# Sixteen accumulating DMAs of a fused encoder block, issued at other places in the program

## The chip, the cores and the metric

The kernel runs on one core of one Trainium2 chip. The metric is the device time of one execution in microseconds (us), and of several executions the median. The core has a matrix engine (TensorE, PE in the profile; its weight loads are shown apart as PEld), three engines for elementwise work (VectorE or DVE, ScalarE or ACT, GpSimd or POOL), and SyncE (SP), which here only issues DMAs. Each engine works through its own queue of instructions in order and waits at semaphores for the others. A DMA is issued from the queue of SP, ACT or POOL and then moved by 16 DMA engines.

## The reference

One layer of an encoder on 512 tokens of width 1024, in float32:

```python
xn = rmsnorm(x, norm_mix_g)
u  = xn @ w_in                       # q | k | v | xr | gr | ga | gb, 1024 columns each
ya = chunked_band_attention(q, k, v, rel_table) @ w_attn_out
yb = (rg_lru(conv(xr)) * gelu(gr)) @ w_rnn_out
h  = x + (sigmoid(ga) * ya + sigmoid(gb) * yb) @ w_o
g, up = split(rmsnorm(h, norm_ffn_g) @ w_ffn_in)     # 2816 columns each
h  = h + (silu(g) * up) @ w_ffn_out
out = rmsnorm(h, final_norm_g)
```

## The kernel before

**Products.** Every float32 product is made of three matmuls (`mm3`, L80 to L82): each operand is split into a rounded high part and a low part, and high by high, high by low and low by high are added up in PSUM. For weights, which come from HBM in blocks of 512 KB, `split` (L84) makes the two parts: ACT copies the high part (L86), then DVE subtracts it from the original (L87), and only then can the matmuls of L81, which read the low part, run.

**Stages in order.** Projections of `w_in` with the recurrence beside them; attention, head by head for 16 heads (`scores`, `transposed`, `weigh`, loop at L1155); the merge, which projects by `w_attn_out` in eight steps (`po_ya`, loop at L1174); the product with `w_o`; the FFN's first projection; the FFN's last projection and the final norm. From `v_all` on PE's order is the program's own.

**The FFN's first projection** runs in six units, `fg0`, `fu0`, `fg1`, `fu1`, `fg2`, `fu2`: the gate and the up columns of three groups (1024, 1024 and 768 columns each). A unit is a seven-product form of a two by two block product (Strassen-Winograd), in the order w11, t1, t2, w22, t3, w21, t4, each of 24 matmuls. The kinds that begin with t multiply sums of weight blocks, which DVE makes at L386, L401 and L407 from blocks that SP loads (L380). A weight of a product is in two halves u=0 and u=1; the matmuls of u=1 begin with the seventh of the product. The weight tiles `whl` have room for two products, so the halves of the next product are made while PE works on this one. Results that are needed again are kept by ACT in SBUF (`kept`, L1310; tiles `keep`, x1, z1 and x2). In the u units DVE adds them to a later bank in place (L1325) and POOL multiplies the sum by the gate (L1326). In the g units ACT applies SiLU (L1319). In `fg1`, `fg2` and the end PE transposes the finished gate products in between (`turn`, L1334).

**The weight sums of the last projection.** The last projection takes the same form over the 2048 rows of `w_ffn_out` that belong to `paired`, which is four groups of two row blocks. Its weight sums are not made on DVE: they are made in DRAM, by DMAs. Per group and kind (t1, t3, t2, t4) `out_copy` (L222, L224) copies a 512 KB block of `w_ffn_out` into a DRAM tile `out_t` from SP's queue, and `out_add` (L226) adds another one to it by an accumulating DMA of 512 KB from POOL's queue (L233). For t1 and t3 what is added is a block of `w_ffn_out`; for t2 it is the finished t1, for t4 the finished t2. That makes 16 copies and 16 adds; `adds` (L236) lists them in the order t1, t3 by groups, then the four t2, then the four t4. The sums are read back (L258 to L267) in the last projection only.

**Where the adds stand.** `step(adds, n, after=...)` (L238) takes the next n from the list. With `after`, `out_add` first has POOL copy one column of the named tile into a small `cell` (L230), and both are kept in the program's order, so that the add is not issued before the tile is there. Before the change four adds are issued in the attention, behind the heads of `ADDS_AT` (no `after`); four in the merge, one with each of its first four steps (L1181, after the tile `mT`); four in `fg1`, behind its products w11, t1, t2 and w22 (`spare_work`, L1419, which asks `ADDS` for the unit and `after` at L1437 for the tile); and four in `fg2` in the same way. The tiles of `after` are the first halves of x1, z1, x2 and of the gate `sg[0, 1]`.

Of the kernel before, what the change touches and what calls it, by code (L numbers as in the profile page):

```python
# [33 lines left out]
N_PLAIN = 3  # L34
GROUP = 2
COPIES = [1] * 16
ADDS_AT = (9, 11, 13, 15)
ADDS = {"fg1": 1, "fg2": 1}
PAIR_TILES = 2 * (11 - N_PLAIN) - (4 - (N_PLAIN - 1))


# [1 line left out]
def block_kernel(ctx: ExitStack, tc: tile.TileContext, x, norm_mix_g, w_in, b_merge, rel_table,  # L43
# [28 lines left out]
    def f(ap):  # L72
        return ap.bitcast(F32)

    def mm_tile(name, tag="mm"):
        return ps.tile([P, S], F32, tag=tag, bufs=4 if tag == "mm" else 2, name=name)
# [7 lines left out]
    def split(hi, lo, src):  # L84

        act.activation(hi, src, AF.Copy)  # L86
        dve.tensor_sub(lo, src, f(hi))  # L87

    def split_pair(o, src):
        split(o[:, 0], o[:, 1], src)  # L90
# [145 lines left out]
    adds = [(out_add, kind, g) for kinds in (("t1", "t3"), ("t2",), ("t4",)) for g in groups for kind in kinds]  # L236

    def step(todo, n=1, **more):  # L238

        for _ in range(min(n, len(todo))):  # L240
            what, *of = todo.pop(0)
            what(*of, **more)
# [207 lines left out]
    def weights(name, ahead=1):  # L450
        prefetch(index[name] + 1 + ahead)
        if index[name] + 1 == len(made):
            low_parts()
        return made[index[name]]

    def project(o, whl, c, xs, lo=0, hi=S):

        n = len(xs)
        for k in range(n):
            at = slice(c * P, (c + 1) * P)  # L460
            mm3(o[:, lo:hi], whl(0, k, at), whl(1, k, at),
                xs[k][:, 0, lo:hi], xs[k][:, 1, lo:hi], k == 0, k == n - 1)
# [80 lines left out]
    def features(pl, tag, name):  # L543

        t = pl.tile([P, KT, 2, S], F32R, tag=tag, name=name)
        return t, [t[:, k] for k in range(KT)]
# [606 lines left out]
    with tc.manual_schedule(engines={mybir.EngineType.PE}):  # L1153
        v_all(sums)
        for h in range(HEADS):  # L1155
# [5 lines left out]
            step(copies, COPIES[h])  # L1161
            if h in ADDS_AT:
                step(adds)
# [6 lines left out]
    m_all, mT = features(xnp, "xn", "mT")  # L1170
# [3 lines left out]
    for j in range(KT):  # L1174
        py = mm_tile(f"po_ya{j}")
        project(py, weights(f"ya{j - j % 2}", 2 if j >= 4 else 1), j % 2, aT)
        dve.scalar_tensor_tensor(ta[j], ta[j], 1.0, py[:], ALU.add, ALU.mult)
        dve.tensor_add(ta[j], ta[j], zB[j])
        at = low_ if j < 4 else every
        split(mT[j][:, 0, at], mT[j][:, 1, at], ta[j][:, at])  # L1180
        step(adds, j < 8 - len(ADDS_AT), after=f(mT[j][:, 0, 0:1]))  # L1181
        if j < 4:
            s3 = tg_.tile([P, 256], F32, tag="tg", name=f"ms3_{j}")
            dve.tensor_sub(s3[:], ta[j][:, low_], ta[j][:, high_])
            split(msT[j][:, 0, high_], msT[j][:, 1, high_], s3[:])
        else:
            i = j - 4
            dve.tensor_add(ta[j][:, high_], ta[i][:, high_], ta[j][:, high_])
            dve.tensor_sub(ta[i][:, low_], ta[j][:, high_], ta[i][:, low_])
            dve.tensor_sub(ta[j][:, low_], ta[j][:, low_], ta[i][:, low_])  # L1190
            split_pair(msT[j], ta[j])
            split(msT[i][:, 0, low_], msT[i][:, 1, low_], ta[i][:, low_])
# [226 lines left out]
    def spare_work(kind):  # L1419
        if unit in ADDS and kind in after:  # L1420
            step(adds, ADDS[unit], after=after[kind])

    for unit in f_units[1:]:
# [13 lines left out]
        after = {"w11": x1[0][:, 0:1], "t1": z1[0][:, 0:1], "t2": x2[0][:, 0:1], "w22": sg[0, 1][:, 0:1]}  # L1437
# [299 lines left out]
```

## Time and profile before

| what | value |
|---|---|
| time, median of 3 runs | 847.2 us |
| the 3 runs | 847.09, 847.20, 848.59 us |
| the profiled execution's own time | 848.82 us |
| its span, first to last instruction | 847.0 us |
| mean granted clock of TensorE | 0.997 |
| DVE, ACT, POOL busy in the span | 654.1, 524.3, 159.9 us |
| DMA, moved in the span | 153.96 MB |

Busy times are of one profiled execution. A row of the timeline gives the start in the span, the length, the engine, the line, the operation, the tile that is written and those that are read, and in brackets the idle time of the engine before it with what ended it. A row of the view by windows gives, for a stretch of the span, the busy time of PE, PEld, DVE, ACT and POOL with the number of instructions, the granted clock, the mean busy share of the 16 DMA engines and GB/s. Buffer numbers are left out of names in the profile, so `keep_fu_x` is x1 or x2 of any u unit, and `out_t` is any of the DRAM tiles.

### The profile page before, as it was taken

How to read it: one execution, taken by the hardware profiler on the slowest of the kernel's cores; microseconds unless marked ns; L12 is line 12 of the kernel's file. 1: busy time of each engine (PE TensorE's matmuls, PEld its weight loads, DVE VectorE, ACT ScalarE, POOL GpSimd, SP SyncE). 2: the span in 40 equal slices, each digit the busy share in tenths (PEclk: the TensorE clock that was granted, in tenths of full speed). 3: DMA queues.
4: the chain of work that ended last, by engine and by line, in shares of the span. 5: the costliest groups of instructions: out<-in, count | busy, mean ns of one | idle time of the engine just before them, and what ended most of it. 6: DMA issues, size and time to landing. Idle time of an engine off the chain costs nothing.

```text
span 847.0 us, 11664 instructions
## 1 busy us (share of the span) xinstructions
PE 837.2 (99%) x4102; PEld 708.8 (84%) x4102; DVE 654.1 (77%) x960; ACT 524.3 (62%) x868; POOL 159.9 (19%) x207
## 2 busy tenths in 40 slices
PE   9999999999999999999999999999999999999996
PEld 6988888888878888888888888888888999988885
DVE  6667779886999778777568777889777878599784
ACT  7595848773456678878544469663765466555543
POOL 2412030221040043343211000005102322200000
PEclk9999999999999999999999999999999999999998
DMA  8433386687565444549448984555955576455442
GB/s 286 166 103 117 130 298 243 212 271 243 167 205 150 132 134 148 157 152 223 94 132 211 320 294 154 157 187 166 229 176 159 150 187 207 140 177 168 160 165 99
DMA packets 104058, 153.96 MB, mean 182 GB/s; under 512 B 8024, under 2 KB 62896, under 8 KB 103488
## 3 DMA queue, kind: packets, MB, share of 16 engines
q1 hardware_dynamic: 99040, 141.32, 51.2%
q0 software_dynamic: 3728, 8.96, 6.4%
q10 hardware_dynamic: 1232, 2.95, 0.9%
q8 instruction: 32, 0.52, 0.3%
q14 instruction: 26, 0.21, 0.1%
HBM read 139.53 MB, written 30.45 MB: 201 GB/s over the span
## 4 chain that ended last, share of the span: by engine, by line
PE 84%; DVE 7%; ACT 4%; DMA 3%; issue 2%; ACTq 0%; DVEq 0%
PE fu_x L80 2%; PE fu_x L81 2%; PE fu_x L82 2%; PE o L1122 2%; PE fg_x L82 2%; PE fg_x L80 2%; PE fg_x L81 2%; PE pT L1102 2%; PE po_ga L82 2%; PE po_ya L80 2%; PE po_ya L82 2%; PE p_out L81 2%; PE p_out L80 2%; PE po_ya L81 2%; PE p_out L82 2%
## 5 line engine op out<-in xcount | busy, mean ns | idle before, releaser
L1326 POOL TENSOR_TENSOR sg<-sg,keep_fu_x 128x512 f32<-128x512 f32 (+1 forms) x10 | 17.8, 1784 | 163.4 <-DVE keep_fu_x L1325 163.4
L1091 POOL TENSOR_SCALAR p<-p,rl 128x128 f32<-128x128 f32 (+3 forms) x61 | 43.8, 733 | 13.7 <-DVE rl L1087 9.4
L1085 DVE CUSTOM_DVE_ANT_0 p<-s,bias 128x128 f32<-128x128 f32 (+1 forms) x64 | 28.6, 486 | 12.6 <-PE s L1077 11.1
L1086 ACT ACTIVATE p<-p,m 128x128 f32<-128x128 f32 (+1 forms) x64 | 35.5, 555 | 2.3 <-DVE m L1085 2.0
L87 DVE TENSOR_TENSOR whl_fu_w<-raw_fu_w,whl_fu_w 128x1024 fp32r<-128x1024 f32 (+1 forms) x18 | 22.1, 1230 | 9.0 <-ACT whl_fu_w L86 9.0
L87 DVE TENSOR_TENSOR pp<-pT,pp 128x384 fp32r<-128x384 f32 (+1 forms) x48 | 26.9, 595 | 2.0 <-ACT pp L86 1.8
L81 PE MATMUL po_xr<-xnT,whl_xr 128*128 128x512 f32 (+1 forms) x80 | 27.7, 354 | 0.0
L87 DVE TENSOR_TENSOR whl_fu_t<-t_fu,whl_fu_t 128x1024 fp32r<-128x1024 f32 (+1 forms) x18 | 23.2, 1293 | 5.9 <-ACT whl_fu_t L86 5.7
L81 PE MATMUL po_gr<-xnT,whl_gr 128*128 128x512 f32 (+1 forms) x80 | 27.5, 347 | 0.0
L82 PE MATMUL po_gr<-xnT,whl_gr 128*128 128x512 f32 (+1 forms) x80 | 27.3, 347 | 0.0
L82 PE MATMUL po_xr<-xnT,whl_xr 128*128 128x512 f32 (+1 forms) x80 | 27.3, 347 | 0.0
L80 PE MATMUL po_gr<-xnT,whl_gr 128*128 128x512 f32 (+1 forms) x80 | 27.2, 347 | 0.0
L738 POOL MEMSET bias<- 64x64 f32 x16 | 2.5, 155 | 130.7 <-DMA bias<-ext_d 130.7
L80 PE MATMUL po_xr<-xnT,whl_xr 128*128 128x512 f32 (+1 forms) x80 | 26.3, 352 | 0.4 <-ACT xnT L649 0.4
L86 ACT ACTIVATE whl_fu_w<-raw_fu_w 128x1024 fp32r<-128x1024 f32 (+1 forms) x18 | 17.7, 987 | 13.0 <-issue 7.1
L80 PE MATMUL po_k<-xnT,whl_qk 128*128 128x512 f32 x64 | 25.5, 398 | 0.0
L80 PE MATMUL po_q<-xnT,whl_qk 128*128 128x512 f32 x64 | 25.5, 398 | 0.0
L80 PE MATMUL po_ga<-xnT,whl_ga 128*128 128x512 f32 x64 | 25.5, 398 | 0.0
L80 PE MATMUL po_gb<-xnT,whl_gb 128*128 128x512 f32 x64 | 25.3, 395 | 0.0
L86 ACT ACTIVATE whl_fu_t<-t_fu 128x1024 fp32r<-128x1024 f32 (+1 forms) x18 | 17.7, 989 | 12.2 <-PE fu_x L82 8.9
L82 PE MATMUL po_ga<-xnT,whl_ga 128*128 128x512 f32 x64 | 25.1, 392 | 0.1
L81 PE MATMUL po_q<-xnT,whl_qk 128*128 128x512 f32 x64 | 25.0, 390 | 0.0
(610 smaller groups left out, 3036.8 us busy)
## 6 DMA issues: line engine op xcount, KB each, us to landing
raw_qk<-in_w_in_dram SPq DMA_DIRECT2D x32, 256.0 KB, 3.3
out_t<-in_w_ffn_out_dram SPq DMA_DIRECT2D x16, 512.0 KB, 5.5
raw_fu_w<-in_w_ffn_in_dram SPq DMA_DIRECT2D x16, 512.0 KB, 4.7
raw_fo<-in_w_ffn_out_dram SPq DMA_DIRECT2D x14, 512.0 KB, 4.3
raw_t<-out_t SPq DMA_DIRECT2D x24, 256.0 KB, 3.3
raw_xr<-in_w_in_dram SPq DMA_DIRECT2D x8, 512.0 KB, 6.0
raw_gr<-in_w_in_dram SPq DMA_DIRECT2D x8, 512.0 KB, 4.5
raw_ga<-in_w_in_dram SPq DMA_DIRECT2D x8, 512.0 KB, 4.9
```

Source lines behind the costliest of these rows:

```text
L80: pe.matmul(o, sh, mh, start=start, stop=False, skip_group_check=parts)
L81: pe.matmul(o, sh, ml, start=False, stop=False, skip_group_check=parts)
L82: pe.matmul(o, sl, mh, start=False, stop=stop, skip_group_check=parts)
L86: act.activation(hi, src, AF.Copy)
L87: dve.tensor_sub(lo, src, f(hi))
L738: pool.memset(b[64:128, 448:512], NEG)
L1085: dve.tensor_tensor_reduce(prob[qb][:], scs[qb][:, 0:w], bias[:, S - w:S], -1.0, 3e38, ALU.add, ALU.min, nmax[:, qb:qb + 1])
L1086: act.activation(prob[qb][:], prob[qb][:], AF.Exp, bias=nmax[:, qb:qb + 1], scale=-1.0, accum_out=lsum[:, qb:qb + 1])
L1091: eng.tensor_scalar(prob[qb][:], prob[qb][:], rl[:, qb:qb + 1], 1.0, ALU.mult, ALU.mult)
L1102: pe.transpose(pt[:, at * P:(at + 1) * P], prob[qb][:, kb * P:(kb + 1) * P], ident[:])
L1122: pe.matmul(po[:, S - n:S], st, pp[i][:, part, lo:lo + n], start=kb == 0 and part == 0, stop=kb == NT - 1 and part == 1)
L1326: (pool if keep and (unit != f_units[-1] or side) else dve).tensor_mul(o, o, keep[a] if keep else banks[a])
```

## The change

```diff
-ADDS_AT = (9, 11, 13, 15)
-ADDS = {"fg1": 1, "fg2": 1}
+ADDS_AT = ()
+ADDS = {"fu0": 1, "fg1": 1, "fu1": 1, "fg2": 1}
...
-        step(adds, j < 8 - len(ADDS_AT), after=f(mT[j][:, 0, 0:1]))
+        step(adds, 0, after=f(mT[j][:, 0, 0:1]))
```

The 16 adds stay what they are and keep their order in the list. No add is left in the attention or in the merge. `fu0` and `fu1` issue four adds each as well, behind their w11, t1, t2 and w22. So `fu0` now holds t1 and t3 of the first two groups, `fg1` those of the last two, `fu1` the four t2, and `fg2` the four t4 as before. PE's rows and SP's rows are the same and in the same order; on ACT and DVE a few neighbours change places in the merge.

POOL's queue in the attention before, from head 13's probabilities on (`p` is a head's probabilities, `bias` its bias tile):

```order
L1091 TENSOR_SCALAR p_2_3826<-p_2_3826,rl_3823 128x384
L233 DMA out_t_3_94<-in_w_ffn_out_dram 256x1x512
L738 MEMSET bias_4021 64x64
L1091 TENSOR_SCALAR p_0_3932<-p_0_3932,rl_3931 128x128
L1091 TENSOR_SCALAR p_1_3933<-p_1_3933,rl_3931 128x256
```

And now at the same place:

```order
L1091 TENSOR_SCALAR p_2_3825<-p_2_3825,rl_3822 128x384
L738 MEMSET bias_4019 64x64
L1091 TENSOR_SCALAR p_0_3930<-p_0_3930,rl_3929 128x128
L1091 TENSOR_SCALAR p_1_3931<-p_1_3931,rl_3929 128x256
L1091 TENSOR_SCALAR p_2_3932<-p_2_3932,rl_3929 128x384
```

The add is gone from between the probabilities.

POOL's queue in `fu0` before (`sg` is the gate of a token block, `keep_fu_x` and `keep_fu_z` the sums that DVE made in place):

```order
L1326 TENSOR_TENSOR sg_0_4935<-sg_0_4935,keep_fu_x_5294 128x512
L1326 TENSOR_TENSOR sg_1_4936<-sg_1_4936,keep_fu_x_5294 128x512
L1326 TENSOR_TENSOR sg_2_4937<-sg_2_4937,keep_fu_z_5295 128x512
L1326 TENSOR_TENSOR sg_3_4938<-sg_3_4938,keep_fu_z_5295 128x512
L1326 TENSOR_TENSOR sg_0_4935<-sg_0_4935,keep_fu_x_5293 128x512
L1326 TENSOR_TENSOR sg_1_4936<-sg_1_4936,keep_fu_x_5293 128x512
```

And now, in the same unit:

```order
L230 COPY cell_t_3_5312<-keep_fu_x_5277 128x1
L233 DMA out_t_3_92<-in_w_ffn_out_dram 256x1x512
L230 COPY cell_t_3_5355<-keep_fu_z_5279 128x1
L233 DMA out_t_3_94<-in_w_ffn_out_dram 256x1x512
L230 COPY cell_t_5_5394<-keep_fu_x_5278 128x1
L233 DMA out_t_5_96<-in_w_ffn_out_dram 256x1x512
L1326 TENSOR_TENSOR sg_0_4919<-sg_0_4919,keep_fu_x_5278 128x512
L1326 TENSOR_TENSOR sg_1_4920<-sg_1_4920,keep_fu_x_5278 128x512
L230 COPY cell_t_5_5437<-sg_0_4919 128x1
L233 DMA out_t_5_98<-in_w_ffn_out_dram 256x1x512
L1326 TENSOR_TENSOR sg_2_4921<-sg_2_4921,keep_fu_z_5279 128x512
L1326 TENSOR_TENSOR sg_3_4922<-sg_3_4922,keep_fu_z_5279 128x512
```

Three cells and adds stand ahead of the first product with the gate, and one of each behind the second.

POOL's queue in `fu1` now, where before only the six products stood:

```order
L230 COPY cell_t_3_5946<-keep_fu_x_5911 128x1
L233 DMA out_t_3_93<-out_t_3_92 128x1024
L230 COPY cell_t_5_5989<-keep_fu_z_5913 128x1
L233 DMA out_t_5_97<-out_t_5_96 128x1024
L230 COPY cell_t_7_6028<-keep_fu_x_5912 128x1
L233 DMA out_t_7_101<-out_t_7_100 128x1024
L1326 TENSOR_TENSOR sg_01_5561<-sg_01_5561,keep_fu_x_5912 128x512
L1326 TENSOR_TENSOR sg_11_5563<-sg_11_5563,keep_fu_x_5912 128x512
L230 COPY cell_t_9_6071<-sg_01_5561 128x1
L233 DMA out_t_9_105<-out_t_9_104 128x1024
```

These four were in `fg1` before; `fg1` now holds four of the form that adds a block of `w_ffn_out`.

## The prediction

> **What bounds the kernel now.** I read the page's first part first, then the view by windows, then the list of PE's waits, and only then the timelines of the units that the change touches.
>
> ```profile
> span 847.0 us, 11664 instructions
> PE 837.2 (99%) x4102; PEld 708.8 (84%) x4102; DVE 654.1 (77%) x960; ACT 524.3 (62%) x868; POOL 159.9 (19%) x207
> ```
>
> PE is busy in 837.2 of 847.0 us. A busy PE could still be one that is fed slowly, so the next two views look for hidden gaps. The rows by windows are the last heads of the attention, the merge, the `w_o` product up to `fg0`, then `fu0`, `fg1`, `fu1` and `fg2`:
>
> ```profile
> 346.00:424.00 78.00, 78.00 (x428) 68.11 (x426) 56.82 (x128) 57.72 (x129) 26.71 (x46) 1.00 0.61 155
> 424.00:475.00 51.00, 51.00 (x229) 42.36 (x229) 38.94 (x62) 23.23 (x34) 6.17 (x8) 1.00 0.70 183
> 475.00:549.00 74.00, 73.80 (x341) 60.84 (x340) 54.67 (x82) 49.86 (x90) 0.00 (x0) 1.00 0.65 227
> 549.00:587.00 38.00, 38.00 (x169) 31.49 (x168) 33.19 (x32) 19.78 (x24) 9.99 (x6) 1.00 0.53 167
> 587.00:629.00 42.00, 42.00 (x203) 35.12 (x202) 32.42 (x32) 26.17 (x37) 5.89 (x9) 1.00 0.75 206
> 629.00:667.00 38.00, 38.00 (x170) 31.51 (x169) 31.05 (x29) 17.90 (x21) 10.90 (x6) 1.00 0.49 150
> 667.00:699.00 32.00, 32.00 (x198) 31.87 (x197) 23.61 (x31) 21.20 (x36) 6.68 (x9) 1.00 0.80 205
> ```
>
> In all of them the granted clock is 1.00 and PE's busy time is the window's length, but for 0.2 us ahead of `fu0`. The DMA share is 0.75 and 0.80 in `fg1` and `fg2`, which hold adds, and 0.53 and 0.49 in `fu0` and `fu1`, which hold none. PE's list of waits has five rows, here the two largest and the last (us in total, times, longest):
>
> ```profile
> PE busy L473 <- DVE eps_t L479: 1.2, 1, 1.2
> PE v_z L81 <- DVE whl_v_t L87: 0.7, 1, 0.7
> ...
> PE pt_mix_0t L647 <- DVE xs_mix L627: 0.2, 1, 0.2
> ```
>
> They lie in the start, in the first scores and in the v product, and asked for 340 to 840 us alone the list is empty. The spacing of matmuls agrees:
>
> ```profile
> 548.94 0.39 PE L80 MATMUL fu_x<-whl_fu_w,hn 128*128 128x512 f32 x1
> 587.02 0.39 PE L80 MATMUL fg_x<-whl_fg_w,hn 128*128 128x512 f32 x1
> ```
>
> From the first matmul of `fu0` to the first of `fg1` are 38.08 us for 7 x 24 = 168 matmuls, 0.227 us each, and neighbours in the timeline stand 0.22 to 0.23 apart. So the kernel is bound by PE's own rate, in the stages that lose adds as well as in those that get them. **There is nothing to win where the adds go away; the question is whether they make PE wait where they arrive.**
>
> **What is removed.** POOL loses four adds in the attention, and four adds with their cells in the merge. The first row is of the form that adds a block of `w_ffn_out` (t1, t3), the second of the form that adds a sum (t2, t4):
>
> ```profile
> L233 POOL DMA_DIRECT2D out_t<-in_w_ffn_out_dram x8: 1032/1046/1107, 379.4 to 460.8; - x8
> L233 POOL DMA_DIRECT2D out_t<-out_t x8: 809/822/850, 591.8 to 688.0; - x8
> ```
>
> That is 8 x 1.05 = 8.4 us of POOL's time, and eight transfers off the DMA engines. PE waits for neither there, so the gain lies between nothing and the 0.2 us of idle PE between 475 and 549 us; I take 0. The few swapped neighbours of ACT and DVE in the merge lie in the 424 to 475 us row, where PE is never idle: 0.
>
> **What is added to POOL's queue.** `fu0` gets four cells and four adds at 1.05 us, `fu1` four cells and four at 0.82. `fg1` keeps four, of the longer form, 4 x 0.23 = 0.9 us more; POOL has nothing else to do there. The t1/t3 form has a habit of its own:
>
> ```profile
> 413.08 1.03 POOL L233 DMA_DIRECT2D out_t<-in_w_ffn_out_dram  x1
> 419.23 1.05 POOL L233 DMA_DIRECT2D out_t<-in_w_ffn_out_dram  x1 [5.12 <-issue]
> DMA to landing us min/median/max: 5.7/5.7/5.7
> DMA to landing us min/median/max: 5.3/6.1/9.6
> ```
>
> The first landing row is that of the add at 413.08, the second that of all sixteen. The add behind it stood ready and started 0.4 us after it had landed (413.08 + 5.7 = 418.8). So such an add holds POOL until the one ahead of it is in, and in `fu0` the adds stand a landing and 0.4 us apart. Bounds for a landing are 5.3 and 9.6; I take the median, 6.1, so 6.5 apart:
>
> ```profile
> 551.86 0.60 ACT L1310 ACTIVATE keep_fu_x<-fu_x 128x512 f32<-128x512 f32 x1 [0.56 <-PE fu_x L82]
> 569.62 0.68 DVE L1325 TENSOR_TENSOR keep_fu_x<-fu_z,keep_fu_x 128x512 f32<-128x512 f32 x1
> 570.45 1.29 POOL L1326 TENSOR_TENSOR sg<-sg,keep_fu_x 128x512 f32<-128x512 f32 x1 [108.57 <-DVE keep_fu_x L1325]
> 575.67 1.29 POOL L1326 TENSOR_TENSOR sg<-sg,keep_fu_z 128x512 f32<-128x512 f32 x1
> ```
>
> x1's first half is kept at 552.5, so with up to 1.2 us for the cell the adds start at about 553.5, 560.0 and 566.5. The third is issued by 567.6, and POOL's first product is not ready until DVE's sum at 570.3. The cell of x2, which DVE's in-place sum at 569.62 now has to wait for, is read behind the second add's issue, which ends at about 561: some 6 us to spare once ACT has kept x2. The fourth add stands between the second and the third product and pushes the third, at 575.67, back by 0.2 + 1.05 = 1.2 us.
>
> **What this does to DVE.** A cell and an issue beside DVE's work look like this in `fg1`:
>
> ```profile
> 590.66 1.22 POOL L230 COPY cell_t<-keep_fg_x 128x1 f32<-128x1 f32 x1 [3.37 <-ACT keep_fg_x L1310]
> 591.83 0.85 POOL L233 DMA_DIRECT2D out_t<-out_t  x1
> 591.77 2.35 DVE L386 TENSOR_TENSOR t_fg<-raw_fg_t,t_fg 128x1024 f32<-128x1024 f32 x2
> ```
>
> DVE makes two subtractions in 2.35 us, as ever: neither cell nor issue costs it anything. POOL's products do. The tightest place of the unit is the second weight half of `fg1`'s w11:
>
> ```profile
> 581.52 1.75 DVE L87 TENSOR_TENSOR whl_fg_w<-raw_fg_w,whl_fg_w 128x1024 fp32r<-128x1024 f32 x1 [1.14 <-ACT whl_fg_w L86]
> 585.09 2.21 POOL L1326 TENSOR_TENSOR sg<-sg,keep_fu_x 128x512 f32<-128x512 f32 x1 [2.90 <-DVE keep_fu_x L1325]
> 586.06 2.32 DVE L87 TENSOR_TENSOR whl_fg_w<-raw_fg_w,whl_fg_w 128x1024 fp32r<-128x1024 f32 x1
> 588.61 0.39 PE L81 MATMUL fg_x<-whl_fg_w,hn 128*128 128x512 f32 x1
> ```
>
> The low half ends at 586.06 + 2.32 = 588.38, and its first matmul is at 588.61: 0.23 us of slack. Of the 2.32 us some 1.1 are POOL's product beside it. DVE idles 1.14 us ahead of 581.52, so all delays up to there are absorbed; behind it, POOL's last two products, shifted by up to 1.2 us, meet other DVE rows than before. Bounds for DVE: 1.1 us less to 1.2 more (one product); for PE: 0 to 1.0 us. Setting the rows one behind the other with the later start, DVE ends 0.1 to 0.2 us later. I take 0.1 us for PE; both ends go into the range.
>
> [...]
>
> **What this does to the loads.** The load that arrives with the least room in a u unit is w21's first block, which DVE needs for L407 ahead of t3's low parts:
>
> ```profile
> 568.48 1.22 DVE L87 TENSOR_TENSOR whl_fu_t<-raw_fu_t,whl_fu_t 128x1024 fp32r<-128x1024 f32 x1
> 572.29 0.39 PE L81 MATMUL fu_x<-whl_fu_t,bts 128*128 128x512 f32 x1
> 645.66 1.23 DVE L407 TENSOR_TENSOR t_fu<-raw_fu_w,t_fu 128x1024 f32<-128x1024 f32 x1 [0.79 <-DMA raw_fu_w<-in_w_ffn_in_dram]
> 649.07 1.22 DVE L87 TENSOR_TENSOR whl_fu_t<-raw_fu_t,whl_fu_t 128x1024 fp32r<-128x1024 f32 x1
> 652.06 0.39 PE L81 MATMUL fu_x<-whl_fu_t,bts 128*128 128x512 f32 x1
> ```
>
> In `fu0` the low half is done at 569.70 for a matmul at 572.29, 2.6 us of slack; in `fu1` at 650.29 for 652.06, 1.8 us. From issue to landing that load takes, in the order of the rows: 3.5 us in `fu0`, 4.7 in `fu1`, 5.4 in `fg2` beside adds; last comes the slowest load beside an add, at 613.4 in `fg1`:
>
> ```profile
> DMA to landing us min/median/max: 3.5/3.5/3.5
> DMA to landing us min/median/max: 4.7/4.7/4.7
> DMA to landing us min/median/max: 5.4/5.4/5.4
> DMA to landing us min/median/max: 7.4/7.4/7.4
> ```
>
> An add beside it in a u unit is not in this trace. Bounds: as now, or 7.4. I take 5.4, the same load of the same step in a unit with adds: 1.9 us later in `fu0`, 0.7 in `fu1`, both inside the slack, 0 us.
>
> **The sum.** 0 + 0.1 + 0. Against the profiled execution's own 848.82 us (span 847.0 and 1.8 around it) that is 848.9; that execution was 1.6 above the median of 847.2, and against the median it is **847.3 us**.
>
> **The rivals.**
>
> *Loads late in both u units (the slower side).* The adds share the DMA engines with w21's loads. At 7.4 us they come 3.9 us later in `fu0` and 2.7 in `fu1`; less the slack that is 1.3 and 0.9 us of PE, 2.2 together: 849.4. It decides from a load of 6.1 us in `fu0` or 6.5 in `fu1`. For it speaks the share of 0.53 that would rise to what `fg1` has. Against it: `fg2` moves its loads and four adds in a shorter unit, and PE does not wait. [...]
>
> *POOL held by its own adds.* If `fu0`'s adds land in 9.6 us, the third starts at about 573.5 and the fourth at 583.5. Four products then fall into 584.5 to 589.7, on top of the tight half: about 0.8 us past it, 0.6 of PE: 847.8. It begins to matter when the first two land 7.5 us after their issue each; the median of sixteen is 6.1.
>
> *A gain where the adds leave.* All idle PE there gone: 0.2 us, 847.0. PE idles too little for more.
>
> That the adds are not moved can be left out: POOL's rows show them at their new places.
>
> **How the numbers follow.** Forecast 0.80, late loads 0.11, POOL held 0.04, small gain 0.05. A measurement tells about 0.2%, 1.7 us, from no change. Only late loads exceed that: slower 0.12 with a little for what I have not seen, faster 0.03 for the same reason, within 0.85. The range goes from the small gain, less 0.3 us because the two lower runs alone lie 0.1 apart, 846.7, to 849.2: the tight half at its bound of 1.0 us and half of the late loads' 2.2.
>
> **What would show it.** Right: PE's list of waits is still empty from 340 to 840 us, `fu0` takes 38.1 us from first matmul to first matmul, the merge's DMA share falls and that of `fu0` rises to about 0.8, and adds in `fu0` start some 6.5 us apart. Wrong: PE rows waiting for DVE at t3 of `fu0` or `fu1` (late loads) or at w11 of `fg1` (products on DVE's path), or a span more than 1 us shorter, which would mean that PE was held in the merge in a way that these views don't show.

## The result, and the profile after

The changed kernel takes **854.12 us** (median of 4 runs, 853.78 to 856.66); the kernel before, beside it, 847.79 us (4 runs, 847.09 to 848.59). The ratio is 1.0078, 95% interval 1.0058 to 1.0097: slower by 6.3 us, where 847.3 and no change were forecast. The profiled execution took 856.66 us.

Span and busy times on the page of the changed kernel:

```profile
span 854.9 us, 11656 instructions
PE 840.7 (98%) x4102; PEld 709.2 (83%) x4102; DVE 660.1 (77%) x960; ACT 523.9 (61%) x868; POOL 167.7 (20%) x211
```

The view by windows of the same stretches as before (the merge, then `fu0`, `fg1`, `fu1` and `fg2`, and last a piece of `fg1`); columns are busy us of PE, PEld, DVE, ACT and POOL, granted clock, DMA share, GB/s. `fu0` begins 2.1 us later than in the trace of before, so these windows cut the units a little earlier:

```profile
424.00:475.00 51.00, 51.00 (x229) 42.35 (x228) 39.47 (x63) 22.69 (x33) 0.00 (x0) 1.00 0.41 133
...
549.00:587.00 38.00, 37.91 (x167) 30.94 (x167) 32.87 (x30) 20.48 (x25) 15.15 (x13) 1.00 0.84 221
587.00:629.00 42.00, 39.83 (x186) 32.78 (x185) 31.96 (x30) 22.89 (x32) 9.64 (x10) 0.96 0.78 201
629.00:667.00 38.00, 38.00 (x169) 31.49 (x168) 30.69 (x27) 19.73 (x24) 12.18 (x12) 1.00 0.74 197
667.00:699.00 32.00, 31.06 (x182) 29.47 (x182) 25.58 (x28) 17.10 (x28) 9.35 (x12) 1.00 0.75 188
...
594.30:597.70 3.40, 3.40 (x9) 2.63 (x8) 3.40 (x4) 0.60 (x1) 1.56 (x2) 0.50 0.99 356
```

The merge has lost its traffic (DMA share 0.70 to 0.41) and PE is as busy there as ever. In the window of `fg1` PE idles 2.2 of 42 us, and for 3.4 us of it the granted clock is 0.50 (the last row). The list of PE's waits for the whole span, largest two rows:

```profile
PE fg_x L81 <- DVE whl_fg_w L87: 3.1, 2, 2.2
PE busy L473 <- DVE eps_t L479: 1.2, 1, 1.2
```

The first row is new: twice, in w11 of `fg1` and of `fg2`, PE waits for a low weight half of DVE's. The time from first matmul to first matmul of each unit, from the timelines:

| unit | before, us | after, us | difference |
|---|---|---|---|
| `fu0` | 38.08 | 38.52 | +0.44 |
| `fg1` | 41.69 | 45.73 | +4.04 |
| `fu1` | 38.08 | 38.08 | 0 |
| `fg2` | 32.67 | 33.91 | +1.24 |
| `fu2` | 30.35 | 30.35 | 0 |

The sum is 5.7 us of the measured 6.3. The two spans differ by 7.9; the rest, 2.1, lies in the first scores, the v product and the `w_o` product (some 0.7 each). The first two come ahead of anything that the change touches, and vary as much between executions of programs that are equal up to there.

**Where `fg1` loses 4 us.** PE's rows around the wait:

```profile
590.96 0.39 PE L80 MATMUL fg_x<-whl_fg_w,hn 128*128 128x512 f32 x1
593.52 0.50 PE L81 MATMUL fg_x<-whl_fg_w,hn 128*128 128x512 f32 x1 [2.17 <-DVE whl_fg_w L87]
...
595.18 0.63 PE L80 MATMUL fg_x<-whl_fg_w,hn 128*128 128x512 f32 x1
595.61 0.63 PE L81 MATMUL fg_x<-whl_fg_w,hn 128*128 128x512 f32 x1
```

The next matmul should stand 0.227 us behind that of 590.96, and stands 2.56 behind: 2.33 us of stall. Some 0.8 us later come eight matmuls that are 0.427 us apart instead of 0.227: 1.6 us more. Together 3.9 of the 4.04.

**Why DVE is late.** The time from issue to landing of w21's first load in `fu0`, issued at 563.2:

```profile
DMA to landing us min/median/max: 6.7/6.7/6.7
```

DVE's rows from there to the half that PE waits for:

```profile
569.99 1.23 DVE L407 TENSOR_TENSOR t_fu<-raw_fu_w,t_fu 128x1024 f32<-128x1024 f32 x1 [2.76 <-DMA raw_fu_w<-in_w_ffn_in_dram]
573.41 1.22 DVE L87 TENSOR_TENSOR whl_fu_t<-raw_fu_t,whl_fu_t 128x1024 fp32r<-128x1024 f32 x1
...
580.76 0.68 DVE L1325 TENSOR_TENSOR keep_fu_z<-fu_x,keep_fu_z 128x512 f32<-128x512 f32 x1
581.36 4.20 DVE L87 TENSOR_TENSOR whl_fu_t<-t_fu,whl_fu_t 128x1024 fp32r<-128x1024 f32 x1
...
587.21 2.31 DVE L386 TENSOR_TENSOR t_fg<-raw_fg_w,raw_fg_w 128x1024 f32<-128x1024 f32 x1
...
591.18 2.29 DVE L87 TENSOR_TENSOR whl_fg_w<-raw_fg_w,whl_fg_w 128x1024 fp32r<-128x1024 f32 x1
```

Before, the first of these rows and the one that now takes 4.20 us stood so:

```profile
565.02 1.22 DVE L407 TENSOR_TENSOR t_fu<-raw_fu_w,t_fu 128x1024 f32<-128x1024 f32 x1
...
578.58 1.21 DVE L87 TENSOR_TENSOR whl_fu_t<-t_fu,whl_fu_t 128x1024 fp32r<-128x1024 f32 x1
```

And POOL's rows in `fu0`, cells, adds and products:

```profile
562.23 1.06 POOL L233 DMA_DIRECT2D out_t<-in_w_ffn_out_dram  x1 [1.53 <-issue]
565.61 0.53 POOL L230 COPY cell_t<-keep_fu_x 128x1 f32<-128x1 f32 x1 [2.31 <-ACT keep_fu_x L1310]
570.09 1.03 POOL L233 DMA_DIRECT2D out_t<-in_w_ffn_out_dram  x1 [3.95 <-issue]
575.31 4.44 POOL L1326 TENSOR_TENSOR sg<-sg,keep_fu_x 128x512 f32<-128x512 f32 x2 [4.18 <-DVE keep_fu_x L1325]
579.70 1.18 POOL L230 COPY cell_t<-sg 128x1 f32<-128x1 f32 x1
580.82 1.07 POOL L233 DMA_DIRECT2D out_t<-in_w_ffn_out_dram  x1
581.42 3.05 POOL L1326 TENSOR_TENSOR sg<-sg,keep_fu_z 128x512 f32<-128x512 f32 x2
```

Two things come together. The second add (562.23, landed 7.5 us behind its issue) moves beside w21's load, which takes 6.7 us instead of 3.5; DVE waits 2.76 us for it and begins L407 late. The rows up to the late half are the same 18 in both kernels, so the delay can be balanced. The fourth cell and add hold POOL for 1.7 us between the x products and the z products. DVE, late and without a pause, has the second z sum ready at 581.44, just as POOL comes to the z products at 581.42, so they run back to back. DVE's row at 581.36 then takes 4.20 instead of 1.21 us: 2.99 us more, about as long as the two products beside it take (3.05). Times in `fu0` behind the unit's first matmul, for the 18 rows of DVE from the first L407 to the second low half of `fg1`'s w11 (worked out from the timelines; the kernels in the lower rows are those of the next section):

| kernel | first L407 | sum of the 18 rows | idle between them | low half done |
|---|---|---|---|---|
| before | 16.07 | 21.97 | 2.44 | 39.43 |
| after | 18.91 | 24.81 | 0 | 42.39 |
| `e4_fourth_last` | 18.71 | 22.42 | 0.38 | 40.23 |
| `e6_pool_alone` | 16.07 | 23.46 | 1.73 | 40.17 |
| `e9_two_in_u` | 16.07 | 22.07 | 2.35 | 39.47 |

The late load brings 2.84 us, the rows that meet POOL's products another 2.84, and DVE had 2.44 us of idle time to pay with. The rows lengthen by so much only where both come together: by 0.45 us with the load alone (`e4`), by 1.49 with the cell and the add alone (`e6`). DVE can pay for most of either, not for both: the half is done 2.96 us late, and `fg1` itself has begun only 0.44 late. (Neighbouring rows overlap by some 0.08 us, so the three columns add up to a little more than the fourth.)

### The profile page after: what moved, and what is told of

It is laid out like the page before. It is cut to its first block, busy times and chain, and to the rows that moved or that the text cites. A ratio compares the mean times of both kernels' runs of the same rounds, so it can differ in the third digit from the quotient of the medians.

```text
span 854.9 us, 11656 instructions
## 1 busy us (share of the span) xinstructions
PE 840.7 (98%) x4102; PEld 709.2 (83%) x4102; DVE 660.1 (77%) x960; ACT 523.9 (61%) x868; POOL 167.7 (20%) x211
## 4 chain that ended last, share of the span: by engine, by line
PE 74%; DVE 11%; DMA 6%; ACT 5%; issue 3%; ACTq 0%; DVEq 0%; SPq 0%
PE o L1122 2%; PE fg_x L81 2%; PE fg_x L82 2%; PE pT L1102 2%; PE fg_x L80 2%; PE po_ga L82 2%; PE po_ya L80 2%; PE po_ya L81 2%; PE p_out L81 2%; PE p_out L80 2%; PE po_ya L82 2%; PE p_out L82 2%; PE po_ga L80 2%; PE po_ga L81 2%; PE po_out L80 2%
## 5 line engine op out<-in xcount | busy, mean ns | idle before, releaser
L1091 POOL TENSOR_SCALAR p<-p,rl 128x128 f32<-128x128 f32 (+3 forms) x61 | 47.3, 792 | 14.0 <-DVE rl L1087 9.3
L230 POOL COPY cell_t<-keep_fu_x 128x1 f32<-128x1 f32 x4 | 2.9, 724 | 165.7 <-ACT keep_fu_x L1310 165.7
L87 DVE TENSOR_TENSOR whl_fu_t<-t_fu,whl_fu_t 128x1024 fp32r<-128x1024 f32 (+1 forms) x18 | 28.7, 1603 | 3.2 <-ACT whl_fu_t L86 3.0
L1326 POOL TENSOR_TENSOR sg<-sg,keep_fu_x 128x512 f32<-128x512 f32 (+1 forms) x10 | 20.4, 2054 | 28.3 <-DVE keep_fu_x L1325 28.3
L80 PE MATMUL po_q<-xnT,whl_qk 128*128 128x512 f32 x64 | 25.5, 398 | 0.0
```

Of the source, the lines that this page charges most:

```text
L80: pe.matmul(o, sh, mh, start=start, stop=False, skip_group_check=parts)
L230: tc.keep_in_program_order(pool.tensor_copy(cell[:, 0:1], after))
L1091: eng.tensor_scalar(prob[qb][:], prob[qb][:], rl[:, qb:qb + 1], 1.0, ALU.mult, ALU.mult)
L1326: (pool if keep and (unit != f_units[-1] or side) else dve).tensor_mul(o, o, keep[a] if keep else banks[a])
```

## The experiments

Each kernel was run beside the kernel before. Ratios are to it, with the 95% interval; its medians were 847.6 to 848.2 us.

**`e1_fu0_only`, `e2_fu1_only`: the adds of one u unit alone.**

```diff
 # e1, against before
-ADDS = {"fg1": 1, "fg2": 1}
+ADDS = {"fu0": 1, "fg1": 1, "fg2": 1}
-        step(adds, j < 8 - len(ADDS_AT), after=f(mT[j][:, 0, 0:1]))
+        step(adds, 0, after=f(mT[j][:, 0, 0:1]))
 # e2, against before
-ADDS = {"fg1": 1, "fg2": 1}
+ADDS = {"fu1": 1, "fg2": 1}
```

> Adds: four in the attention as before, none in the merge, four each in fu0, fg1 and fg2. If what costs is the four adds in fu0 (late loads, POOL's order, or both), the time is about 4 us above the kernel before: some 2.3 us of PE waiting at w11 of fg1 and 1.6 us of slow matmuls behind it, 851.5 to 852. If the emptied attention costs something by itself, that part is missing here and the time is lower than that. If the adds in fu1 carried most of it, the time is within 1 us of before.

> Adds: four in the attention and four in the merge as before, then four in fu1 and four in fg2, none in fg1. If fu1 costs by itself what the changed kernel's trace shows (a wait of 1.1 us at w11 of fg2, no slow matmuls behind it), the time is 1.0 to 1.3 us above the kernel before, and fg1, now without adds, gives nothing back since PE never waited there. If fu1 was late only because fu0 had been, it is the same as before.

`e1` 851.42 us (849.45 to 853.76), 1.0028 [1.0011, 1.0046]; `e2` 849.57 us (847.5 to 855.13), 1.0022 [1.0001, 1.0043]. PE's list of waits, `e1` first and then `e2`, one fence each:

```profile
PE fg_x L81 <- DVE whl_fg_w L87: 2.2, 1, 2.2
```

```profile
PE fu_x L81 <- DVE whl_fu_t L87: 2.4, 1, 2.4
```

With `fu0` as the only u unit that holds adds the wait at w11 of `fg1` is there in full, so it comes from `fu0`'s own adds, not from those in `fu1` or from the emptied attention. In the profiled `e1` no half clock follows it: the granted clock is 1.00 from 586 to 596 us. In `e2` the loads beside the adds came later still (7.1 and 9.5 us from issue), and t3 of `fu1` itself waited; the wait at w11 of `fg2` that was expected is not there. The profiled `e2` is one of its longer executions (853.76 us), so this trace shows more than its median lost. Both parts cost something; `fu0` costs more by the medians, but the intervals overlap.

**`e3_merge_eight`: the attention emptied alone**, its four adds into the merge (`ADDS_AT = ()`, the rest as before).

> Adds: none in the attention, eight in the merge, four each in fg1 and fg2. The theory that only the arrival in the u units costs: same as the kernel before, within 1 us. The rival that the emptied attention shifts DVE and PE there (the changed kernel's trace has about 1 us more in the v product and 0.6 us in the product with w_o): 1 to 2 us above.

850.54 us (849.22 to 852.84), 1.002 [1.0004, 1.0035]. The units of the FFN are as before. In the profiled execution, the longest of the ten, the time goes in the `w_o` product:

```profile
PE o_z L82 <- DVE ms L87: 3.0, 1, 3.0
```

Eight adds in the merge bring a wait of their own, so this run does not show what an emptied attention does by itself. `e8` does that.

**`e8_first_eight_out`: the kernel before without its first eight additions.** It leaves these out of the sums (`ADDS_AT = ()`, the list from the ninth on, none in the merge).

> The kernel before without its first eight adds (four in the attention, four in the merge), which it leaves out; fg1 and fg2 as before. That is what the change takes away, alone. Theory that there is nothing to win there: same as before within 1 us. A rival in which their traffic or POOL's time held PE: 1 to 2 us below before. A rival in which the emptied queue shifts other work to a worse place (0.4 us in the product with w_o in the changed kernel's trace): 0.5 to 1.5 us above.

847.89 us (847.05 to 849.52), 0.9996 [0.9986, 1.0006]. Where the adds leave there is nothing to win.

**`e5_traffic_alone`, `e6_pool_alone`: the two causes apart.** In `e5` the eight DMAs of the u units are plain copies of 512 KB from ACT's queue, without cells, so eight additions are left out; in `e6` cells and adds stand where the change puts them but move two rows each, so most of eight additions is left out.

```diff
 # e5, against after, in out_add
+        if by_act:
+            tc.keep_in_program_order(act.dma_start(out=out_t[kind, g[0]][0][:], in_=what))
+            return
 # e6, against after, in out_add
+        if tiny:
+            to = out_t[kind, g[0]][0]
+            tc.keep_in_program_order(pool.dma_start(out=to[0:2], in_=what[0:2], accum_op=ALU.add, max_dma_last_dim=4096))
+            return
```

> The changed kernel, but the eight adds of fu0 and fu1 are plain copies of the same 512 KB from ACT's queue, without cells: the transfers beside the weight loads stay, POOL has only its six products. It leaves those eight additions out. Theory POOL order: POOL's products meet DVE as in the kernel before, so w11 of fg1 and of fg2 wait 0.5 us or less, and the time is at most 1.5 us above before, the rest being t3 late by its load. Theory late loads: w21's first block still lands 5.5 us or more after its issue, DVE is 2 us late, w11 of fg1 still waits 1.5 us or more, and the time is 3 us or more above before.

> The changed kernel, but each of the eight adds of fu0 and fu1 moves two rows instead of the whole block: cells and issues stay in POOL's queue at their places, the traffic goes. It leaves most of those eight additions out. Theory late loads: w21's first block lands 3.5 to 4.7 us after its issue, DVE is on time, nothing waits, and the time is that of before within 1 us. Theory POOL order: the fourth cell and issue still push the two z products together and the row of DVE beside them still takes about 4 us, so that w11 of fg1 waits 1 us or more and the time is 1.5 to 4 us above before. If both are needed, the z products are pushed together but DVE has the 2.8 us that the loads cost in the changed kernel, and the wait is under 0.5 us.

`e5` 848.15 us (847.09 to 849.43), 0.9998 [0.9987, 1.001]; `e6` 848.5 us (847.72 to 854.18), 1.0016 [0.9998, 1.0033]. `e5` is a weak test: beside plain copies w21's load took 4.8 us, not 6.7, and DVE's L407 was 0.9 us late, not 2.8. `e6` is a better one: the loads are on time, and the cell and the add still stand between the products (this kernel's line numbers are up to four higher):

```profile
575.42 0.18 POOL L230 COPY cell_t<-sg 128x1 f32<-128x1 f32 x1
575.54 0.86 POOL L235 DMA_DIRECT2D out_t<-in_w_ffn_out_dram  x1
576.14 1.58 POOL L1330 TENSOR_TENSOR sg<-sg,keep_fu_z 128x512 f32<-128x512 f32 x1
579.50 2.21 POOL L1330 TENSOR_TENSOR sg<-sg,keep_fu_z 128x512 f32<-128x512 f32 x1 [1.77 <-DVE keep_fu_z L1329]
```

With DVE on time the second z product is not yet ready when the first is done, so the two stand apart, and w11 of `fg1` waits 0.56 us by the spacing of its matmuls. The interval of `e6` includes no change at all. Its profiled execution is the longest of the ten (852.4 us of span), with 2.1 us of wait at t3 of `fg2`, a place that the edit does not touch.

**`e4_fourth_last`: the late load without POOL's order.** In the u units the fourth cell and add go behind the unit's last product:

```diff
+        if unit[1] == "u":
+            after["t4"] = sg[1, 0][:, 0:1]
+            del after["w22"]
```

> The changed kernel with the fourth add of fu0 and of fu1 behind POOL's six products instead of between the second and the third. Theory POOL order (the fourth add pushes the two z products together and they hold DVE off for 4.2 us): the wait at w11 of fg1 falls from 2.3 us to 0.5 or less, the slow matmuls behind it go, fu1's wait of 1.1 us goes too, and the time is 848 to 849.5. Theory late loads (w21's first block arrives 6.7 us after its issue instead of 3.5, and DVE never makes it up): DVE is still late at w11, the wait stays at 1.5 us or more, and the time is 852 or more.

849.67 us (848.54 to 852.53), 1.0022 [1.0007, 1.0037]. DVE's first L407 waits for its load as in the changed kernel, POOL's products run without a cell between them, and PE's longest wait at w11 of `fg1` is 0.3 us:

```profile
566.86 1.23 DVE L407 TENSOR_TENSOR t_fu<-raw_fu_w,t_fu 128x1024 f32<-128x1024 f32 x1 [2.55 <-DMA raw_fu_w<-in_w_ffn_in_dram]
...
578.23 1.71 DVE L87 TENSOR_TENSOR whl_fu_t<-t_fu,whl_fu_t 128x1024 fp32r<-128x1024 f32 x1
```

```profile
PE fg_x L81 <- DVE whl_fg_w L87: 0.3, 1, 0.3
```

The 4.20 us row is 1.71 here. The two z products follow each other without a gap here too, but take 4.51 us instead of 3.05, with DVE's rows of 1.71 and 0.68 us beside them; why DVE's row grows to 4.20 us in the changed kernel and not here these runs do not show. `e4` is 1.5 us above the kernel before, where the changed kernel is 6.3 above, with all sixteen additions made and the loads nearly as late as there. What is left is spread: in the profile `fu0`, `fg1`, `fu1` and `fg2` take 0.2, 0.6, 0.6 and 0.3 us more than before. The median lies 0.2 us above the range expected.

**`e7_changed_again`: the changed kernel once more.**

> The changed kernel itself once more, beside the others on the same chip: 853.5 to 854.5 us, 0.6 to 0.8% above before, with the wait at w11 of fg1 between 2 and 2.6 us. If the slow matmuls behind that wait are there in some executions only, the times have two groups about 1.6 us apart.

855.06 us (854.48 to 857.77), 1.0086 [1.0059, 1.0113]. The stall of 2.35 us at w11 of `fg1` is there again, with the half clock behind it (0.83 in the mean from 586 to 596 us); in this execution, the longest of the four, t3 of `fg2` waited 2.4 us as well. The median is 0.6 us above what was expected, and the four times do not show two groups.

**`e9_two_in_u`: both causes avoided.** Four adds stay in the attention, none in the merge, `fu0` and `fu1` get two each (behind x1 and behind the last product), `fg1` and `fg2` four each.

```diff
 # against after
-ADDS_AT = ()
+ADDS_AT = (9, 11, 13, 15)
+        if unit[1] == "u":
+            after = {"w11": x1[0][:, 0:1], "t4": sg[1, 0][:, 0:1]}
```

> The additions are placed so that neither cause is there: four stay in the attention, none in the merge, fu0 and fu1 get two each (one behind x1 of w11, whose addition has landed before w21's loads are issued, one behind the unit's last product, so that no cell stands between POOL's products), fg1 and fg2 four each. Theory (late load and POOL's order together make the wait): fu0 38.1 to 38.3 us, no wait of over 0.5 us at w11 of fg1 and of fg2, no matmuls at 0.427 us in fg1, time 847.8 to 848.8, the same as before. Rival (any addition in a u unit costs, by its traffic in this stretch): about half of what the changed kernel costs, 850 to 852, with waits of 1 us and more in fu0, fg1, fu1 or fg2.

848.02 us (846.63 to 850.03), 1.0003 [0.9989, 1.0016]. The unit is back at 38.08 us and PE never waits in it, with a DMA share above the 0.53 of before:

```profile
549.00:587.00 38.00, 38.00 (x169) 31.46 (x168) 33.28 (x32) 19.76 (x24) 11.95 (x8) 1.00 0.60 180
```

So a u unit can carry two adds for nothing where they stand so. `e9` changes the places and halves the number, so how much each of the two does is not shown; that the place counts is what `e4` shows. It is no gain either.

**`e10_busy_pe`: PE busy instead of waiting.** The changed kernel with ten matmuls into a bank that nobody reads, at the place of the wait:

```diff
+                if (unit, kind, a, k) == ("fg1", "w11", 0, 2):
+                    spin = mm_tile("spin", "s")
+                    for _ in range(10):
+                        pe.matmul(spin[:, 0:f_side(unit)], src[:, 0, 0, at], w(0, 0), start=True, stop=True)
```

> The changed kernel, and in w11 of fg1 ahead of the third of its four k steps ten matmuls more into a bank that nobody reads, 2.27 us of PE, so that PE is busy where it waited 2.33 us. Theory (the idle 2.3 us bring the half clock behind it): the wait falls under 0.3 us, the matmuls behind it take 0.227 us and none 0.427, fg1 takes about 44.1 instead of 45.7 us, time 852.0 to 853.5, some 1.6 below the changed kernel. Rival (the clock is halved for something else in that stretch, such as what DVE, POOL and the DMA engines do there): the wait is gone, but 8 or so matmuls still take 0.427 us, time as the changed kernel's, 854 to 856. A second rival, that the added matmuls push everything back and the wait stays, would show 2.3 us more: 856.5.

852.55 us (850.6 to 854.86), 1.0065 [1.0046, 1.0083]. `fg1` takes 44.17 us instead of 45.73, and the window shows PE busy throughout at the full clock:

```profile
586.00:600.00 14.00, 14.00 (x69) 11.41 (x69) 11.90 (x11) 8.00 (x11) 4.44 (x4) 1.00 0.90 253
```

DVE is as late as in the changed kernel (the low half done 42.47 us behind `fu0`'s first matmul), and yet in this window the granted clock is 1.00 and no matmul behind that place stands 0.427 us from the one before it. That fits 1.6 us for the lower clock behind the stall of 2.33 us, and the medians agree (1.6 below the one run of the changed kernel, 2.5 below the other). It is not proof: the intervals of the ratios overlap, and the profiled `e1` had the idle PE without the half clock and took 44.22 us for `fg1`.

## Why the prediction was wrong

**What bounds the kernel, and nothing to win where adds leave: right.** The merge is as full of PE's work as before, and `e8` is level.

**POOL's queue: nearly right.** The habit of this form of add, to hold POOL until the one ahead has landed, was there: 562.23 + 7.5 is 569.7, and the third starts at 570.09. The adds stood 6.7 and 7.9 us apart, not 6.5. The third is still ahead of POOL's first product, as forecast.

**Loads, the first half of the failed step.** "An add beside it in a u unit is not in this trace", with 5.4 us taken; it took 6.7, inside the bounds. The 5.4 came from one execution: w21's two loads in `fg2` took 4.6 to 9.2 us in the traces of the other runs, with the same adds in that unit. The error was the next sentence: "both inside the slack, 0 us". That slack, 2.6 us, was the distance to PE's matmul in t3, and PE did wait little there (0.25 us by the spacing of its matmuls). But DVE stood still for 2.76 us in that wait, and began what followed 2.84 us later. With the 5.4 us that were taken it would have been 1.9, less than the 2.44 us that DVE idles behind it. A delay that PE does not see is not gone; it goes along DVE's queue to the next tight place.

**DVE, the second half, and the step that failed: "DVE idles 1.14 us ahead of 581.52, so all delays up to there are absorbed".** The bound for PE, 0 to 1.0 us with 0.1 taken, was worked out for POOL's shift of one product with DVE on time. That is what `e6` measured, and 0.56 us lies inside it. With the load's delay added there was no idle time left (0 of 2.44), and one row of DVE, beside two products in a row, took 4.20 us instead of 1.21; all 18 rows took 2.84 us more. The place was named rightly, the two delays that meet there were never added up. The measured wait is 2.33 us, against a bound of 1.0.

The forecast's bound of one product, 1.2 us more for DVE, was the author's estimate. The row that took 4.20 us, 2.99 more than before, stood beside two products of together 3.05: the worst case should have been both of the products that POOL had ready.

**The half clock was not in the sum.** The forecast had no price for a lower clock behind a stall of PE, since the trace of before shows neither in these stages. In the profiled execution the granted clock was 0.50 for 3.4 us, and eight matmuls at 0.427 us added 1.6 us to 2.33.

**The rivals.** "Loads late" had the landing right (6.7, past its threshold of 6.1), but priced it at t3, where little of it shows. "POOL held by its own adds" had products falling on the tight half, at 0.6 us of PE. What came is both, neither of them alone: `e4` and `e6` lie 1.5 and 0.4 us over the kernel before by the medians (1.9 and 1.4 by the ratios), the change 6.3. `fu1` repeats it on a smaller scale: its first L407 comes 1.25 us later in the unit, the row beside its two z products takes 3.94 us, and w11 of `fg2` waits 0.9 us. (The upper end of the forecast range, added up from its terms, is 849.3 and not 849.2; that changes nothing.)

**What would show it wrong** was named: PE rows that wait for DVE at w11 of `fg1`, "products on DVE's path". They are what came. The DMA share of `fu0` came as forecast, 0.84 for about 0.8.

What stays open: 0.6 us between the units' sum and the medians, and the waits at t3 of `fg2` that some executions show (1.1 us in `e1`, 2.1 in `e6`, 2.4 in `e7`). Their traces show what is late there: w21's two loads, which land 5.0 to 5.4 us after issue before, take 7.1 to 9.2 in these three, and DVE waits for them. Why they do so in some executions is not known.

## What to carry to other kernels

When a change delays one engine twice, put both delays on the same ledger: take the engine's rows from the first delay to the next tight place, add the delays, and subtract its idle time once. Slack measured to the consumer does not bring back the time of the producer. Here an add and a tiny copy between two products on POOL cost 0.56 us of PE's time while DVE was on time, and 2.33 when DVE was late; behind the last product, as in `e4` and `e9`, they cost less or nothing: PE's longest wait at w11 of `fg1` was 0.3 us in `e4`, and `e9` has none there.

## What the runs showed of the hardware

- **Behind five of seven stalls of PE, of 2.3 to 3.2 us, matmuls stood nearly twice as far apart for some 3 us.** Matmuls 0.427 instead of 0.227 us apart came behind stalls of 2.33 us (after), 2.35 (`e7`), 2.6 (`e2`) and 3.2 (`e3`), and narrower ones 0.32 instead of 0.17 apart behind 2.3 at t3 of `fg2` in `e6`; none came behind 2.35 in `e1` or 2.6 at t3 of `fg2` in `e7`. In the changed kernel the granted clock was 0.50 from 594.30 to 597.70 us, 3.4 us, and 1.00 in the rest of its trace up to PE's last matmul, as in the whole trace of before up to there. What decides it is not shown: 2.33 us of stall had it behind them in the changed kernel, 2.35 in `e1` did not. The first rows behind the stall in `e3`, 0.80 and 0.63 long where 0.39 is usual:

```profile
484.05 0.80 PE L82 MATMUL o_z<-whl_o_t,ms 128*128 128x512 f32 x1 [3.01 <-DVE ms L87]
484.64 0.63 PE L80 MATMUL o_z<-whl_o_t,ms 128*128 128x512 f32 x1
```
- **An accumulating DMA from POOL's queue was a heavier neighbour than a copy of its size from ACT's.** The same load took 3.5 us with neither beside it (before), 4.8 beside a plain copy of 512 KB (`e5`) and 6.5 to 6.7 beside an accumulating one (`e4`, after). Whether the adding or the queue makes the difference is not shown.
